# Offsets of the weight parts and the order of their matmuls in 55 gate and value units

## The chip, the cores and the metric

The kernel runs on one core of a Trainium2 chip. The metric is the device time in microseconds of one execution. The time before is the median of two runs.

## What is computed

One layer of a bidirectional encoder on 256 tokens of width 2048, in float32: an RMS norm, a combined projection, a windowed attention beside a Fourier mix, an output projection, and then the feed-forward part, with which this change deals. In the reference it reads:

```python
def _conv_ffn(h, w_up, dw_w, dw_b, w_down):
    up = h @ w_up
    gate, val = up[..., :D_FF], up[..., D_FF:]
    gate = lax.conv_general_dilated(
        gate, dw_w, window_strides=(1,), padding=((CONV_WIDTH // 2, CONV_WIDTH // 2),),
        dimension_numbers=('NWC', 'WIO', 'NWC'), feature_group_count=D_FF) + dw_b
    act = jax.nn.gelu(gate, approximate=False) * val
    return act @ w_down
...
x = x + _conv_ffn(_rmsnorm(x, norm2_g), w_up, dw_w, dw_b, w_down)
```

D_FF is 5504, which is 43 tiles of 128 features, so there are 43 gate tiles and 43 value tiles.

## The kernel before

Every float32 matrix is split in two parts of the type float32r: a high part, which ScalarE copies (L163), and a low part, which VectorE makes by subtracting the high part from the original (L164). A product is then the sum of high by high, high by low and low by high.

A **unit** is one tile of weights: for a gate or a value tile, 128 partitions by 2048 elements, which holds 16 stationary blocks of 128 by 128. `load` (L143) brings it in on SP's queue into one of three `raw` buffers. `split` (L156) makes its two parts in tiles `hi` and `lo`, three buffers each, 2176 elements wide, of which `parts_of` (L149) takes 2048 from an offset that the list `shifts` gives. The offset was 16 for the first eight units and 0 for all others.

`still_weights` (L303) multiplies a unit. The weights stand still in the array and the tokens move: `hk(k)` is block k of the normed, transposed input (the tiles `hU`), 512 elements wide, of which the first 256 are the high parts of the 256 tokens and the second 256 their low parts. First come 16 matmuls with the high weights on all 512 columns (L310), then 16 with the low weights on the first 256 columns (L313), all of them into one PSUM bank. ScalarE and VectorE add the two halves of the bank behind it (`scaled_sum`, L824 to L827), and the gate goes on through the convolution and the GELU.

The feed-forward part is a list of **items** (`ff_items`, L68): the gate and value units of tiles 0 to 7 first, then four groups that follow `PATTERN`: three units, then a down-projection product and a unit in turn. In it `u` is a unit and `s` a product (12 matmuls of 512 columns, `by_parts`, L1038), made for the tiles of the group before. After the groups come the last units and the rest of the down-projection. One loop (L1122) goes through the list. For each item it issues the matmuls and then `ff_step(n)`, which issues, in this order, the work on the item before (such as `scaled_sum`), the split of item n + 2 with the load that its buffer allows, and the work that may come behind. So the tiles of an item are written about two items ahead, and each of the two rings of three holds the item at work and the two that follow it. The order on each engine is written out by hand.

Of the kernel before, what the change touches and what calls it, by code (L numbers as in the profile page):

```python
# [13 lines left out]
P = 128  # L14
D = 2048
S = 256
NK = D // P
# [50 lines left out]
def ff_items():  # L68


    def ups(tiles):
        return [(kind, j) for j in tiles for kind in ("gate", "val")]

    items = ups(range(8))
    for g in range(N_GROUPS):
        todo = {
            "u": ups(range(8 * g + 8, 8 * g + 16)),
            "s": [("product", g, c, p) for c in range(2) for p in PRODUCTS[c]],
        }
        items += [todo[c].pop(0) for c in PATTERN]  # L80
        assert not any(todo.values())
    items += [("down", 0, c) for c in range(4)] + ups(LAST)
    items += [("down", 1, c) for c in range(4)] + [("last", c) for c in range(4)]
    return items
# [3 lines left out]
def block_kernel(  # L88
# [18 lines left out]
    nc = tc.nc  # L107
# [10 lines left out]
    def bank(pool, name):  # L118
        return pool.tile([P, 512], F32, tag=pool.name, name=name)
# [4 lines left out]
    shifts = [(SHIFT, SHIFT)] * 8 + [(0, 0)] * 32  # L124
    n_front = len(units)
    items, up_index = ff_items(), {}
    for n, it in enumerate(items):
        if it[0] == "product":
            continue
        up_index[n] = len(units)  # L130
        if it[0] in ("gate", "val"):
            units.append((w_up[2 * it[1] + (it[0] == "val")], 2048))
            shifts.append((0, 0))
            continue
        elif it[0] == "down":
            units.append((w_down_late[4 * it[1] + it[2]], 2048))
        else:
            units.append((w_down_last[it[1]], 512 * len(LAST)))
        shifts.append((0, 0))
    RAW = 3  # L140
    raws, halves = {}, {}
# [7 lines left out]
    def parts_of(i):  # L149
        halves[i] = tuple(  # L150
            wp.tile([P, 2176], F32R, tag=h, name=f"{h}{i}", bufs=3)[:, s : s + 2048]
            for h, s in zip(("hi", "lo"), shifts[i])
        )
        return halves[i]

# [43 lines left out]
    def u_part(k, o, n, m=1):  # L199

        rows = ux[k // 4][:, (k < 4) * U_HEAD :].rearrange("p (k c) -> p k c", k=4)
        return rows[:, k % 4 : k % 4 + m, o : o + n]
# [39 lines left out]
    ps = bank(dn, "ps_warm")  # L242
# [48 lines left out]
    def moving_weights(hi, lo, n, kk, act, b, ps, first, last, q0=0):  # L291

        for q, k in enumerate(kk, q0):
            ah = act(k)[:, b * P : (b + 1) * P]
            al = act(k)[:, S + b * P : S + (b + 1) * P]
            wh, wl = hi[:, q * n : (q + 1) * n], lo[:, q * n : (q + 1) * n]
            nc.tensor.matmul(ps, ah, wh, start=first and q == q0, stop=False)  # L297
            nc.tensor.matmul(ps, al, wh, start=False, stop=False)  # L298
            nc.tensor.matmul(  # L299
                ps, ah, wl, start=False, stop=last and q == q0 + len(kk) - 1  # L300
            )

    def still_weights(hi, lo, ps, kk):  # L303

        for k in kk:
            s = slice(k * P, (k + 1) * P)
            nc.tensor.matmul(ps, hi[:, s], hk(k), start=k == 0, stop=False)  # L310
        for k in kk:
            s = slice(k * P, (k + 1) * P)
            nc.tensor.matmul(  # L313
                ps[:, 0:S], lo[:, s], hk(k)[:, 0:S], start=False, stop=k == NK - 1
            )

    def hk(k):
        return hT[k // 4][:, k % 4, :]
# [18 lines left out]
    def at(when, i, f, *a):  # L337
        when.setdefault(i, []).append((f, a))
# [17 lines left out]
    for k in range(NK):  # L356
        c, q = k // 4, k % 4
        if q == 0:
            hi, lo = (t.rearrange("p (k c) -> p k c", k=4) for t in parts_of(c))
        n = 1 if c < 2 else 2  # L360
# [3 lines left out]
        if q % n == 0:  # L364
            w, h = u_part(k, 0, FW, n), hi[:, q : q + n, :]
# [3 lines left out]
        if k < 4:  # L369

            for p, w in enumerate([hi, hi, lo]):
                for b in range(2):
# [3 lines left out]
                        start=k == 0 and p == 0, stop=False,  # L376
# [405 lines left out]
    for n, (c, kq) in enumerate(OUT_ORDER):  # L782
        i = N_OUT + n
# [14 lines left out]
        if kq >= 2:  # L798
            part = "a" if kq == 2 else "f"
            ps = ps_a[c] if kq < 3 else ps_a[c, "f"]  # L800
# [113 lines left out]
    def ring_load():  # L914
        if ring_next[0] < len(ring):
            key = ring[ring_next[0]]
            ring_next[0] += 1
            ring_tiles[key] = fp.tile([P, 2048], F32, tag="rawd", name="rawd%d%d%s" % key)
            nc.sync.dma_start(ring_tiles[key], weights_of(*key))
# [24 lines left out]
    def first_sums(g, c):  # L944

        a, b = ring_tiles[g, c, "a"], ring_tiles[g, c, "b"]
        x = ring_tiles["x"] = fp.tile([P, 2048], F32, tag="sumw", name=f"sumw{g}{c}", bufs=1)
        nc.vector.tensor_tensor(x, a, b, ALU.add)
        nc.gpsimd.dma_start(b, weights_of(g, c, "d"), accum_op=ALU.add)
# [14 lines left out]
    def ff_step(n):  # L964
        todo, later[:] = list(later), []
        for f in todo:
            next(f, None)
        run(beside, n)
        split_item(n + 2)
        for f in todo:  # L970
            for _ in f:
                pass
        run(behind, n)

    def up_posts(n, kind, j, ps):
        if kind == "gate":
            at(beside, n + 1, scaled_sum, ps, f"g{j}")
            at(beside, n + 2, gate_conv, j)
            at(behind, n + 2, gate_gelu, j)
        else:  # L980
            at(beside, n + 1, scaled_sum, ps, f"v{j}")
            at(beside, n + 2, val_mult, j)
            if j % 8 == 7 and j < 8 * N_GROUPS:
                g = j // 8
                at(behind, n + 1, operand, g, "P1")
                at(behind, n + 2, operand, g, "N4")
                at(behind, n + 3, operand_sums, g, 0)
                at(behind, n + 4, operand, g, "P7")
                at(behind, n + 4, operand, g, "P2")
                at(behind, n + 5, operand_sums, g, 1)  # L990
                at(behind, n + 5, operand, g, "N5")
                at(behind, n + 6, operand, g, "N3")
                at(behind, n + 7, operand, g, "P6")
            if j >= 8 * N_GROUPS:
                at(behind, n + 2, act_parts, j)
# [42 lines left out]
    def by_parts(ps, o, hi, lo, first, last):  # L1038

        for p in range(4):  # L1040
            s = slice(p * 512, (p + 1) * 512)
            nc.tensor.matmul(ps, o[:, 0, p, :], hi[:, s], start=first and p == 0, stop=False)  # L1042
            nc.tensor.matmul(ps, o[:, 1, p, :], hi[:, s], start=False, stop=False)  # L1043
            nc.tensor.matmul(ps, o[:, 0, p, :], lo[:, s], start=False, stop=last and p == 3)  # L1044
# [59 lines left out]
    for q in range(2):  # L1104
        kind, j = items[q]
        ps = bank(mm, f"ps_{kind}{j}")
# [6 lines left out]
    for ps, hi, lo in pair:  # L1113
        still_weights(hi, lo, ps, range(12, NK))
# [7 lines left out]
    for n, it in enumerate(items):  # L1122
        if n < 2:
            continue
        if it[0] == "last":
            break
        if n in (8, 9):
            ring_load()
        if n == 13:
            pending.append(lambda: first_sums(0, 0))  # L1130
        if it[0] in ("gate", "val"):
            kind, j = it
            ps = bank(mm, f"ps_{kind}{j}")
            still_weights(*halves.pop(up_index[n]), ps, range(NK))
            ff_step(n)
            up_posts(n, kind, j, ps)
            continue
        if it[0] == "product":
            kind, g, c, p = it
            end = g == N_GROUPS - 1  # L1140
            if (c, p) in held:
                by_parts(held[c, p], parts[p], *halves.pop(it), g == 0, end)
            else:
                ps = bank(mm, f"ps_{p}{g}{c}")
                by_parts(ps, parts[p], *halves.pop(it), True, True)
                at(beside, n + 1, product_out, g, c, p, ps)
            if end and p == "N4":
                for q in range(3):
                    at(behind, n + 1 + q, shared_out, c, q)
        else:  # L1150
            kind, g, c = it
            hi, lo = halves.pop(up_index[n])
            ps = [bank(mm, f"ps_l{g}{c}{b}") for b in range(2)]
            for b in range(2):
                moving_weights(hi, lo, 512, LATE[g], act.get, b, ps[b], True, True)
            at(beside, n + 1, down_out, c, ps)
            if (g, c) == (0, 0):
                gfb = fp.tile([P, D], F32, tag="sumw", name="gfb", bufs=1)
                nc.gpsimd.dma_start(gfb, normf_g.partition_broadcast(P))
        ff_step(n)  # L1160
# [3 lines left out]
    i = up_index[n]  # L1164
# [149 lines left out]
```

## Time and profile before

| | us |
|---|---|
| median of the runs | 956.09 (955.68 to 956.5) |
| the profiled execution | 956.12 |
| its span | 954.4 |
| mean granted TensorE clock | 0.997 |

The span goes from the first to the last instruction of the profiled execution; the time also holds what lies around it. PE is TensorE's matmuls and PEld its weight loads, DVE is VectorE, ACT ScalarE, POOL GpSimd and SP the queue that issues most loads. L310 is line 310 of the kernel before. Times within the trace count from the start of the span. The feed-forward units begin at about 257 us and the four groups with products end at about 853 us. A matmul's record lasts longer than the distance to the next matmul, since matmuls are pipelined; the price of one in a stream is the distance from start to start.

### The profile page before, as it was taken

The numbers are of one execution on the slowest core, as the hardware profiler recorded it, in microseconds if no ns is written. First come the engines' busy times: TensorE is split into PE (matmuls) and PEld (weight loads), VectorE is DVE, ScalarE is ACT, GpSimd is POOL, SyncE is SP. The second block draws the span as 40 slices with busy tenths as digits, with TensorE's granted clock in tenths as the row PEclk, the third lists the DMA queues.
The fourth block names the chain that finished last, engine by engine and source line by source line (L and its number), as shares of the span: only waits on it lengthen the run. The fifth ranks groups of instructions, "written<-read, shape, count | busy, mean of one in ns | idle before, by whom it ended". The sixth has DMA issues, their size and how long they took to land.

```text
span 954.4 us, 12779 instructions
## 1 busy us (share of the span) xinstructions
PE 944.7 (99%) x5085; PEld 814.4 (85%) x5085; DVE 750.7 (79%) x935; ACT 534.2 (56%) x646; POOL 43.3 (5%) x58
## 2 busy tenths in 40 slices
PE   9999999999999999999999999999999999999996
PEld 7888998888888888888888888888888888888885
DVE  7658877566576689787898978988779979888775
ACT  7656766454454446556565555655556755554442
POOL 0000000000000000000000000000000000000003
PEclk9999999999999999999999999999999999999998
DMA  9844444446546676977778797876977687776442
GB/s 366 332 184 149 160 146 163 148 166 216 177 176 235 250 220 192 289 235 260 227 255 245 237 303 226 265 248 210 292 247 251 205 293 221 219 243 217 177 133 89
DMA packets 32108, 211.58 MB, mean 222 GB/s; under 512 B 3504, under 2 KB 4016, under 8 KB 7984
## 3 DMA queue, kind: packets, MB, share of 16 engines
q1 hardware_dynamic: 28448, 184.55, 52.2%
q0 software_dynamic: 3600, 26.22, 14.6%
q8 instruction: 40, 0.66, 0.3%
q14 instruction: 20, 0.16, 0.0%
HBM read 208.65 MB, written 2.10 MB: 221 GB/s over the span
## 4 chain that ended last, share of the span: by engine, by line
PE 98%; DVE 1%; DMA 0%; issue 0%; ACT 0%; POOL 0%; POOLq 0%; DVEq 0%; ACTq 0%
PE ps_gate L310 17%; PE ps_val L310 17%; PE ps_val L313 8%; PE ps_gate L313 8%; PE ps_q L310 5%; PE ps_P L1042 3%; PE ps_P L1043 3%; PE ps_P L1044 3%; PE ps_q L313 2%; PE ps_N L1042 2%; PE ps_N L1043 2%; PE ps_a L299 2%; PE ps_a L297 2%; PE ps_a L298 2%; PE ps_N L1044 2%; PE ps_k L310 2%
## 5 line engine op out<-in xcount | busy, mean ns | idle before, releaser
L164 DVE TENSOR_TENSOR lo<-raw,hi 128x2048 fp32r<-128x2048 f32 (+1 forms) x133 | 302.7, 2276 | 54.8 <-ACT hi L163 54.8
L163 ACT ACTIVATE hi<-raw 128x2048 fp32r<-128x2048 f32 (+1 forms) x133 | 253.1, 1903 | 59.9 <-PE ps_l L298 24.8
L310 PE MATMUL ps_gate<-hU,hi 128*128 128x512 f32 x688 | 165.5, 392 | 0.0
L310 PE MATMUL ps_val<-hU,hi 128*128 128x512 f32 x688 | 165.2, 392 | 0.0
L310 PEld LDWEIGHTS ps_gate<-hU,hi 128*128 128x128 f32 x688 | 128.1, 188 | 27.6
L310 PEld LDWEIGHTS ps_val<-hU,hi 128*128 128x128 f32 x688 | 128.0, 188 | 27.3
L313 PEld LDWEIGHTS ps_val<-hU,lo 128*128 128x128 f32 x688 | 85.4, 188 | 3.7
L313 PEld LDWEIGHTS ps_gate<-hU,lo 128*128 128x128 f32 x688 | 84.6, 188 | 3.8
L313 PE MATMUL ps_val<-hU,lo 128*128 128x256 f32 x688 | 86.2, 277 | 0.0
L824 ACT ACTIVATE ft_g<-ps_gate 128x256 f32<-128x256 f32 x43 | 16.5, 384 | 123.1 <-PE ps_gate L313 123.1
L313 PE MATMUL ps_gate<-hU,lo 128*128 128x256 f32 x688 | 85.2, 276 | 0.0
L824 ACT ACTIVATE ft_v<-ps_val 128x256 f32<-128x256 f32 x43 | 16.5, 385 | 92.7 <-PE ps_val L313 92.7
L1043 PE MATMUL ps_P<-hi_P,op_P 128*128 128x512 f32 x128 | 50.2, 392 | 0.0
L1042 PE MATMUL ps_P<-hi_P,op_P 128*128 128x512 f32 x128 | 50.1, 392 | 0.0
L1044 PE MATMUL ps_P<-lo_P,op_P 128*128 128x512 f32 x128 | 49.8, 389 | 0.0
L310 PE MATMUL ps_q<-hT,hi 128*128 128x512 f32 x192 | 46.5, 394 | 0.0
L934 DVE TENSOR_TENSOR lo_N<-sumw,hi_N 128x2048 fp32r<-128x2048 f32 x16 | 36.6, 2290 | 10.1 <-ACT hi_N L933 10.1
L310 PEld LDWEIGHTS ps_q<-hT,hi 128*128 128x128 f32 x192 | 35.2, 188 | 7.0
L826 DVE TENSOR_TENSOR fa_g<-ps_gate,ft_g 128x256 f32<-128x256 f32 x43 | 18.2, 423 | 26.1 <-ACT ft_g L824 26.1
L297 PE MATMUL ps_a<-hi,cat 128*128 128x512 f32 x96 | 37.9, 395 | 0.0
L1043 PE MATMUL ps_N<-hi_N,op_N 128*128 128x512 f32 x96 | 37.6, 392 | 0.0
L1042 PE MATMUL ps_N<-hi_N,op_N 128*128 128x512 f32 x96 | 37.6, 392 | 0.0
(332 smaller groups left out, 1561.4 us busy)
## 6 DMA issues: line engine op xcount, KB each, us to landing
raw<-in_w_up SPq DMA_DIRECT2D x86, 1024.0 KB, 5.2
raw<-in_w_in SPq DMA_DIRECT2D x20, 1024.0 KB, 4.8
raw<-in_w_out SPq DMA_DIRECT2D x16, 1024.0 KB, 4.9
sumw<-in_w_down POOLq DMA_DIRECT2D x16, 1024.0 KB, 8.7
raw<-in_w_down_late SPq DMA_DIRECT2D x8, 1024.0 KB, 4.8
raw<-in_w_down_last SPq DMA_DIRECT2D x4, 768.0 KB, 4.2
ux<-in_w_u_x SPq DMA_DIRECT2D x3, 768.0 KB, 9.3
xs<-in_x SPq DMA_DIRECT2D x4, 512.0 KB, 16.4
```

The source lines that it names most:

```text
L163: nc.scalar.activation(hi[:, 0:n], raw[:, 0:n], AF.Copy)
L164: nc.vector.tensor_tensor(lo[:, 0:n], raw[:, 0:n], f32(hi[:, 0:n]), ALU.subtract)
L297: nc.tensor.matmul(ps, ah, wh, start=first and q == q0, stop=False)
L298: nc.tensor.matmul(ps, al, wh, start=False, stop=False)
L299: nc.tensor.matmul(ps, ah, wl, start=False, stop=last and q == q0 + len(kk) - 1)
L310: nc.tensor.matmul(ps, hi[:, s], hk(k), start=k == 0, stop=False)
L313: nc.tensor.matmul(ps[:, 0:S], lo[:, s], hk(k)[:, 0:S], start=False, stop=k == NK - 1)
L824: nc.scalar.activation(tmp, ps[:, S : 2 * S], AF.Copy)
L934: nc.vector.tensor_tensor(lo, src, f32(hi), ALU.subtract)
L1042: nc.tensor.matmul(ps, o[:, 0, p, :], hi[:, s], start=first and p == 0, stop=False)
L1043: nc.tensor.matmul(ps, o[:, 1, p, :], hi[:, s], start=False, stop=False)
L1044: nc.tensor.matmul(ps, o[:, 0, p, :], lo[:, s], start=False, stop=last and p == 3)
```

## The change

The units that directly follow a down-projection product, 55 in number, each get an entry of a list `kinds`: the offset of the high part in its tile, the offset of the low part, a group size, and whether the order is turned in every second group. All other units, and the products, stay as they are. With a group size of `NK` (16) the order is the old one; with 2, two high matmuls are followed by the two low ones of the same blocks; with 1, high and low alternate. The low matmul of a block still uses 256 columns and the high one 512.

```diff
+    steps = (0, 16, 32, 48)
+    kinds = [(a, b, g, False) for g in (NK, 2, 1) for a in steps for b in steps]
+    kinds += [(0, 0, 1, True), (16, 0, 1, True), (0, 0, 8, False), (0, 0, 4, False)]
+    kinds += [(4, 4, NK, False), (60, 60, NK, False), (20, 20, NK, False)]
+    kind_of = {}
     for n, it in enumerate(items):
...
         if it[0] in ("gate", "val"):
             units.append((w_up[2 * it[1] + (it[0] == "val")], 2048))
-            shifts.append((0, 0))
+            if items[n - 1][0] == "product" and kinds:
+                kind_of[n] = kinds.pop(0)
+            shifts.append(kind_of.get(n, (0, 0)))
             continue
...
-            for h, s in zip(("hi", "lo"), shifts[i])
+            for h, s in zip(("hi", "lo"), shifts[i][:2])
...
-    def still_weights(hi, lo, ps, kk):
-        for k in kk:
-            s = slice(k * P, (k + 1) * P)
-            nc.tensor.matmul(ps, hi[:, s], hk(k), start=k == 0, stop=False)
-        for k in kk:
-            s = slice(k * P, (k + 1) * P)
+    def still_weights(hi, lo, ps, kk, group=NK, turn=False):
+        order = []
+        for n, k0 in enumerate(kk[::group]):
+            ks = range(k0, min(k0 + group, kk[-1] + 1))
+            for w in (lo, hi) if turn and n % 2 else (hi, lo):
+                order += [(w, k) for k in ks]
+        for n, (w, k) in enumerate(order):
+            x = slice(0, S if w is lo else 2 * S)
             nc.tensor.matmul(
-                ps[:, 0:S], lo[:, s], hk(k)[:, 0:S], start=False, stop=k == NK - 1
+                ps[:, x], w[:, k * P : (k + 1) * P], hk(k)[:, x],
+                start=n == 0 and k == 0, stop=n == len(order) - 1 and k == NK - 1,
             )
...
-            still_weights(*halves.pop(up_index[n]), ps, range(NK))
+            still_weights(
+                *halves.pop(up_index[n]), ps, range(NK), *kind_of.get(n, (0, 0, NK, False))[2:]
+            )
```

An offset counts elements of four bytes.

## The prediction

> **What bounds the kernel now.** I read the page first, then what TensorE waited for, then the chain of waits around the changed units, then single stretches of the timeline.
>
> ```profile
> span 954.4 us, 12779 instructions
> ...
> PE 944.7 (99%) x5085; PEld 814.4 (85%) x5085; DVE 750.7 (79%) x935; ACT 534.2 (56%) x646; POOL 43.3 (5%) x58
> ...
> PEclk9999999999999999999999999999999999999998
> ...
> PE 98%; DVE 1%; DMA 0%; issue 0%; ACT 0%; POOL 0%; POOLq 0%; DVEq 0%; ACTq 0%
> ```
>
> TensorE is busy for 99% of the span at a full granted clock, and 98% of the chain that ended last is its own matmuls. Its waits, all of them:
>
> ```profile
> PE ps_warm L244 <- POOL ones L236: 1.0, 1, 1.0
> PE ps_u L374 <- ACT hT L251: 0.2, 1, 0.2
> ```
>
> After the start it waits for nobody, so only two things can move the time: the distance from one matmul's start to the next, and a new wait. The change touches 55 of the 86 gate and value units. The chain of waits shows five groups of matmuls, with start, length and count:
>
> ```profile
> 352.74 3.66 PE ps_val L310 x16
> 356.40 1.88 PE ps_val L313 x16
> 358.28 3.68 PE ps_gate L310 x16
> 361.96 1.81 PE ps_gate L313 x16
> ...
> 366.52 3.68 PE ps_val L310 x16
> 370.20 1.81 PE ps_val L313 x16
> ```
>
> L310 is the product with the high parts (512 columns), L313 the one with the low parts (256 columns). The unit at 366.52 follows a down-projection product, as all 55 do. It takes 3.68 + 1.81 = 5.49 us: 230.0 ns for a high matmul, 113.1 ns for a low one, 343.1 ns for a pair of the two. The unit at 352.74 follows another unit, does the same work with tiles at the same offsets, and has 228.8 and 117.5 ns. So one shape has more than one price, and the price depends on what ran before. That is the ground on which this change plays. Two neighbouring streams bound it:
>
> ```profile
> 133.88 0.71 PE ps_o L688 x6
> 134.60 0.72 PE ps_s L616 x6
> ...
> 852.66:874.42 21.76, 21.76 (x97) 18.02 (x96) 21.13 (x23) 8.10 (x6) 0.00 (x0) 1.00 0.65 228
> ```
>
> The first two rows (chain of waits) are 256-column matmuls of the attention, 118.3 and 120 ns each. The third is a stretch of 96 matmuls of 512 columns into ps_l (97 touch it): us, then each engine's busy time, and 21.76 / 96 = 226.7 ns, the shortest steady price that I see for that width.
>
> ```profile
> 500.76 0.39 PE L1044 MATMUL ps_P<-lo_P,op_P 128*128 128x512 f32 x1
> 500.99 1.10 PE L310 MATMUL ps_gate<-hU,hi 128*128 128x512 f32 x4
> ...
> 501.93 0.62 PE L310 MATMUL ps_gate<-hU,hi 128*128 128x512 f32 x2
> ```
>
> This is the timeline of a unit that starts behind a product: its first four high matmuls begin at 500.99 and the fifth at 501.93, which is 235 ns each. The start of a new stream is its slowest part.
>
> **The change part by part.** It adds no instruction and removes none: each unit keeps 16 high and 16 low matmuls of the same widths, one ScalarE copy, one VectorE subtraction and one load. The 55 units, by their list: 16 keep the old order with offsets of 0, 16, 32 or 48 elements of the high and the low part (the first of these is the old unit); 16 with the same offsets go in groups of two high, two low; 16 alternate high and low; two alternate with the order turned in every second pair; one goes by eights, one by fours; three keep the order with offsets of 4, 60 and 20. So 34 units, 34 x 16 = 544 pairs, are interleaved, and 20 others are changed in the offset or hardly in the order.
>
> Offsets, on the writers:
>
> ```profile
> L164 DVE TENSOR_TENSOR lo<-raw,hi x3: 2292/2293/2293, 24.4 to 37.7; 128x2048 fp32r<-128x2048 f32 x3
> ...
> L163 ACT ACTIVATE hi<-raw x4: 1901/1911/1918, 22.4 to 39.2; 128x2048 fp32r<-128x2048 f32 x4
> ...
> L164 DVE TENSOR_TENSOR lo<-raw,hi x15: 2281/2284/2293, 370.4 to 477.6; 128x2048 fp32r<-128x2048 f32 x15
> ...
> L163 ACT ACTIVATE hi<-raw x15: 1902/1913/1924, 367.4 to 473.5; 128x2048 fp32r<-128x2048 f32 x15
> ```
>
> The rows are minimum, median and maximum ns. Before 40 us the tiles already stand at offset 16, after 366 us at 0: the medians are 2293 against 2284 and 1911 against 1913 ns. I cost an offset of whole sixteens at nothing there. TensorE's lack of waits hides a few ns more.
>
> Offsets, on the reader: no row shows a stationary operand at another offset. The bounds are the two prices of a low group, 1.81 and 1.88 us. All 55 units have the lower one now, so an offset can hardly help there and can cost 0.07 us a unit. I take one unit in four flipped: 20 x 0.07 / 4 = 0.35 us, with 0 and 1.4 as ends. The offsets of 4, 60 and 20 have no near row; their three units stand in the same term.
>
> Interleaving, the new wait: the low part is needed at the second or third matmul of a unit instead of the seventeenth.
>
> ```profile
> 497.48 2.29 DVE L164 TENSOR_TENSOR lo<-raw,hi 128x2048 fp32r<-128x2048 f32 x1
> ```
>
> This low part is complete at 499.77, and its unit starts at 500.99. It is 1.22 us early, the tightest of the 55 that I found. The move costs nothing. If VectorE came 1.3 us later, each unit would wait, with the next matmuls of TensorE, and everything after, queued behind.
>
> Interleaving, the release of tiles: the high tile is now read until the end of its unit, about 1.8 us longer.
>
> ```profile
> L824 ACT ACTIVATE ft_g<-ps_gate 128x256 f32<-128x256 f32 x43 | 16.5, 384 | 123.1 <-PE ps_gate L313 123.1
> ```
>
> The next writer of that tile is ScalarE's copy for the item three places on. It is issued behind L824, which itself waits for the unit's last matmul, as its row says. So ScalarE could not use the earlier release, and nothing is lost. The loads on SP's queue keep their order and hang on the same copies and subtractions; GpSimd's accumulating loads hang on the products' tiles, which don't change.
>
> Interleaving, on the array: before, a unit had one switch from high to low; now it has 31 (alternating), 15 or 16. What a switch does to the weight load is seen at the old borders:
>
> ```profile
> 358.01 3.52 PEld L310 LDWEIGHTS ps_gate<-hU,hi 128*128 128x128 f32 x16
> ...
> 358.12 3.84 PE L310 MATMUL ps_gate<-hU,hi 128*128 128x512 f32 x16
> ```
>
> Here a high matmul follows the last low one. Its weights begin to load 0.11 us ahead, which is the whole length of that low matmul, and the matmul starts as soon as it ends. The short matmul still covers the load, so no load is uncovered by alternating. What is left is the price of each matmul in a stream that keeps switching: for the high ones between 226.7 and 235 ns, for the low ones between 113.1 and 120 ns, a pair between 339.8 and 355 ns against 343.1 now. That is -1.8 to +6.5 us over 544 pairs. I take the high ones as they are, and the low ones half way between the two prices of their own group, 115.3 ns, because the lower one has so far come only in an unbroken run of low matmuls: 2.2 x 544 = 1.2 us.
>
> **Sum.** +1.2 + 0.35 = +1.55 us on the profiled execution's 956.12 us, whose span is 954.4, with 1.7 us around it that nothing here touches. It lies 0.03 us from the median of the runs, 956.09. I forecast 957.7 us.
>
> **The rivals.** *Order and offset don't matter* (chance 0.17): the load and the stream don't meet, the times of the changed units stay 5.49 us, and the kernel stays at 956.1. For it: the writers' rows, and the border at 358. Against it: the same group at 1.81 and 1.88 us. The Trainium skill says this outright ("TensorE: Matmul & The Clock Gate", section "Step-by-step: what each phase is for"): TensorE has two independent read ports, so that loading the next tile's weights takes no read bandwidth from the running matmul. By that rule a matmul's price would be fixed by its columns; this case's trace has 226.7 to 235 ns for 512 of them, so I don't follow it for the small terms.
>
> *The streams fall into step* (0.17): both kinds of matmul go at their shortest, 16 x 226.7 ns + 1.81 us = 5.437 us a unit instead of 5.49. The gain is 0.053 x 55 = 2.9 us: 953.2. For it: the ps_l run stays at 226.7 with a new pair of operands at each step. Against it: 16 high matmuls in a row never reach it now.
>
> *Every switch is a start* (0.12): high matmuls stay at the 235 ns of a unit's beginning and low ones at 120. 11.9 x 544 = 6.5 us, and the offsets' upper end 1.4: 964.0. This is slower than before, by 0.8%. For it: the first matmuls behind a product are the slow ones. Against it: the unit at 352.74 begins after a low group and has the lower 3.66 us.
>
> *The load of the high weights is laid bare* (0.02): if a high load could not run beside a low matmul, each pair would pay the 0.11 us between the load at 358.01 and its matmul at 358.12: 0.11 x 544 = 59.8 us, 1015.9. This is the rival of the other sign that passes 2%. It decides from 19.1 / 544 = 35 ns of uncovered load per pair. The rows at 358 speak against it.
>
> The forecast has 0.52, its own range 955.9 to 961. To leave out no more than two in ten I take half of the falling-into-step case and half of the every-switch case in: 954.0 to 962.5. Two per cent, about what a measurement of this kernel can tell from no change, is 19 us: only the laid-bare load passes it, 0.02; for a gain of that size no case is left, 0.01 for what I don't see; within it 0.97.
>
> **What would show it.** Right: the interleaved units at 5.45 to 5.65 us, the low matmuls among them spaced between 113 and 120 ns, no wait of TensorE behind L164, and most units of the old order at 5.49 or 5.54 whatever their offset. In-step shows as 5.44 us in most units, every-switch as 5.68. Wrong: a unit beyond 5.7 us, TensorE waiting for VectorE or ScalarE, or offsets of one kind that all lie apart from the others.

## The result, and the profile after

The changed kernel takes 961.50 us (961.50 to 961.51, two runs), against 956.09 before: a ratio of 1.0056, with a 95% interval of 1.004 to 1.0072. That is a slowdown of half a per cent, far inside the two per cent, and 5.4 us where the forecast had 1.6. The time lies inside the stated 954.0 to 962.5 us, and 0.5 us above the forecast's own range of 955.9 to 961. The profiled execution also took 961.50 us.

The page after:

```profile
span 959.7 us, 12779 instructions
...
PE 950.0 (99%) x5085; PEld 818.9 (85%) x5085; DVE 750.7 (78%) x935; ACT 534.2 (56%) x646; POOL 43.4 (5%) x58
...
PE 98%; DVE 1%; DMA 0%; issue 0%; ACT 0%; POOL 0%; POOLq 0%; DVEq 0%; ACTq 0%
```

The instructions are as many as before, VectorE and ScalarE are busy exactly as long, and the 5.3 us of the span stand on TensorE alone (944.7 before). Its waits:

```profile
PE ps_warm L253 <- POOL ones L245: 1.0, 1, 1.0
PE ps_u L388 <- ACT hT L260: 0.3, 1, 0.3
```

No wait was added. So the matmuls themselves stand further apart. The two matmul lines of `still_weights` have become one, L326, and the chain of waits now merges the 32 matmuls of a unit into one piece (start, length, what). The pieces shown are, in order: old order with offsets 0/0, 0/16, 0/32, 16/0, 16/16 and 32/16 (high/low); twos with 0/0; alternating with 0/0, 0/16 and 0/32; and the last one, old order with 20/20.

```profile
366.82 5.50 PE ps_val L326 x32
...
375.06 5.60 PE ps_gate L326 x32
...
383.41 5.51 PE ps_val L326 x32
...
399.99 5.55 PE ps_val L326 x32
...
408.29 5.58 PE ps_gate L326 x32
...
441.62 5.66 PE ps_gate L326 x32
...
511.23 5.55 PE ps_val L326 x32
...
655.80 5.59 PE ps_val L326 x32
...
664.13 5.46 PE ps_gate L326 x32
...
672.34 5.54 PE ps_val L326 x32
...
849.89 5.52 PE ps_val L326 x32
```

The first unit is the old unit and has the old length. Nearly all others are longer, the ones that kept their order too. All 48 that combine the four offsets, in us from the unit's first matmul to the next item's:

| order | high offset | low 0 | low 16 | low 32 | low 48 |
|---|---|---|---|---|---|
| old | 0 | 5.495 | 5.599 | 5.508 | 5.577 |
| old | 16 | 5.553 | 5.583 | 5.557 | 5.602 |
| old | 32 | 5.628 | 5.656 | 5.631 | 5.636 |
| old | 48 | 5.600 | 5.636 | 5.543 | 5.611 |
| twos | 0 | 5.554 | 5.590 | 5.630 | 5.603 |
| twos | 16 | 5.549 | 5.570 | 5.595 | 5.604 |
| twos | 32 | 5.548 | 5.679 | 5.575 | 5.619 |
| twos | 48 | 5.622 | 5.645 | 5.624 | 5.596 |
| alternating | 0 | 5.588 | 5.461 | 5.539 | 5.550 |
| alternating | 16 | 5.599 | 5.549 | 5.564 | 5.595 |
| alternating | 32 | 5.636 | 5.470 | 5.639 | 5.611 |
| alternating | 48 | 5.655 | 5.624 | 5.563 | 5.600 |

Over 5.495 us, the 16 of the old order cost 1.50 us together, the twos 1.68, the alternating ones 1.32, the other seven 0.43. That is 4.93 of the 5.4 us; the products behind the units add 0.1, and the feed-forward part began 0.3 us later than in the profile of before, behind a part that the change leaves alone.

Where a unit's time goes is seen in the timeline, for units with 0/0, 0/16, 16/0 and 20/20 in the old order (start, length, and the start of the product behind them):

```profile
366.66 3.84 PE L326 MATMUL ps_val<-hU,hi 128*128 128x512 f32 x16 
370.34 1.98 PE L326 MATMUL ps_val<-hU,lo 128*128 128x256 f32 x16 
...
372.16 0.39 PE L1056 MATMUL ps_P<-hi_P,op_P 128*128 128x512 f32 x1 
...
374.90 3.84 PE L326 MATMUL ps_gate<-hU,hi 128*128 128x512 f32 x16 
378.58 2.08 PE L326 MATMUL ps_gate<-hU,lo 128*128 128x256 f32 x16 
...
380.50 0.39 PE L1056 MATMUL ps_N<-hi_N,op_N 128*128 128x512 f32 x1 
...
399.83 3.83 PE L326 MATMUL ps_val<-hU,hi 128*128 128x512 f32 x16 
403.50 2.04 PE L326 MATMUL ps_val<-hU,lo 128*128 128x256 f32 x16 
405.38 0.39 PE L1056 MATMUL ps_P<-hi_P,op_P 128*128 128x512 f32 x1 
...
849.73 3.79 PE L326 MATMUL ps_val<-hU,hi 128*128 128x512 f32 x16 
853.36 2.05 PE L326 MATMUL ps_val<-hU,lo 128*128 128x256 f32 x16 
855.25 0.39 PE L1056 MATMUL ps_N<-hi_N,op_N 128*128 128x512 f32 x1 
```

The high matmuls take 3.68 us in the first two, the low ones 1.82 with the low part at 0 and 1.92 at 16. The unit with 20/20 has its high ones at 3.63 us, 226.7 ns each, which is the shortest steady price of before, but its low ones at 1.89. So each offset moves its own half of the unit, up or down. The low half depends on the high offset as well: with 16/0 the low part is at 0 again, as in the old unit, and its matmuls take 1.88 us instead of 1.82.

### The profile page after: what moved, and what is told of

It is laid out like the page before. It is cut to its first block, busy times and chain, and to the rows that moved or that the text cites. A ratio compares the mean times of both kernels' runs of the same rounds, so it can differ in the third digit from the quotient of the medians.

```text
span 959.7 us, 12779 instructions
## 1 busy us (share of the span) xinstructions
PE 950.0 (99%) x5085; PEld 818.9 (85%) x5085; DVE 750.7 (78%) x935; ACT 534.2 (56%) x646; POOL 43.4 (5%) x58
## 4 chain that ended last, share of the span: by engine, by line
PE 98%; DVE 1%; DMA 0%; issue 0%; ACT 0%; POOL 0%; POOLq 0%; DVEq 0%; ACTq 0%
PE ps_val L326 25%; PE ps_gate L326 25%; PE ps_q L326 7%; PE ps_P L1056 3%; PE ps_P L1057 3%; PE ps_P L1058 3%; PE ps_k L326 2%; PE ps_N L1056 2%; PE ps_N L1058 2%; PE ps_N L1057 2%; PE ps_a L308 2%; PE ps_a L306 2%; PE ps_a L307 2%; PE ps_l L307 2%; PE ps_l L308 2%; PE ps_l L306 2%
## 5 line engine op out<-in xcount | busy, mean ns | idle before, releaser
L326 PE MATMUL ps_gate<-hU,hi 128*128 128x512 f32 x688 | 190.9, 393 | 0.0
L326 PE MATMUL ps_val<-hU,hi 128*128 128x512 f32 x688 | 190.5, 393 | 0.0
L326 PEld LDWEIGHTS ps_gate<-hU,hi 128*128 128x128 f32 x688 | 123.6, 188 | 22.1
L326 PEld LDWEIGHTS ps_val<-hU,hi 128*128 128x128 f32 x688 | 123.6, 188 | 22.1
L326 PE MATMUL ps_val<-hU,lo 128*128 128x256 f32 x688 | 117.8, 280 | 0.0
L326 PE MATMUL ps_gate<-hU,lo 128*128 128x256 f32 x688 | 117.4, 279 | 0.0
L326 PEld LDWEIGHTS ps_gate<-hU,lo 128*128 128x128 f32 x688 | 103.6, 188 | 9.3
L326 PEld LDWEIGHTS ps_val<-hU,lo 128*128 128x128 f32 x688 | 103.9, 188 | 8.9
L326 PE MATMUL ps_q<-hT,hi 128*128 128x512 f32 x192 | 46.5, 394 | 0.0
L326 PEld LDWEIGHTS ps_q<-hT,hi 128*128 128x128 f32 x192 | 35.2, 188 | 7.0
L1056 PE MATMUL ps_N<-hi_N,op_N 128*128 128x512 f32 x96 | 37.6, 392 | 0.0
L1058 PE MATMUL ps_N<-lo_N,op_N 128*128 128x512 f32 x96 | 37.6, 391 | 0.0
```

What stands on the lines that cost most here:

```text
L326: nc.tensor.matmul(ps[:, x], w[:, k * P : (k + 1) * P], hk(k)[:, x], start=n == 0 and k == 0, stop=n == len(order) - 1 and k == NK - 1,)
```

## The experiments

Three questions were open: whether offsets or order cost the time, whether a unit's time is its own or comes from its neighbours, and what about an offset counts. Unless said otherwise, unit times and prices of a matmul are distances from start to start in the trace of the run. A **rhythm** is a sequence of such distances that repeats, and **dear** and **cheap** stand for long and short. Times of kernels are medians; where an interval is given, the ratio is to the kernel before on the same chip. The kernels for which no time is given ran once, and only their traces are read.

**Offsets alone, order alone.** In the first kernel all 55 units have the old order, in the second all have offset 0.

```diff
+    kinds = [(a, b, NK, False) for a, b, g, t in kinds]
```

> All 55 units keep the old order, each with the offsets of its entry. If a unit's time is its own, set by its offsets and its order wherever it stands, the 16 offset pairs cost what they cost in the trace of the changed kernel (together 1.50 us over 16 old units), now three times, with 0.24 us for the rest: 956.1 + 4.7 = 960.8 us, and the pair of offsets 0 and 16 is again about 5.60 us a unit. If the switches between high and low cost the time, only the 19 units that had kept the order stay dear: 957.8 us.

```diff
+    kinds = [(0, 0, g, t) for a, b, g, t in kinds]
```

> All 55 units at offset 0, each in the order of its entry. If a unit's time is its own, the units in twos cost 0.06 us and the alternating ones 0.09 us over 5.495, as the ones at offset 0 do in the trace of the changed kernel, and with the last few the sum is 2.7 us: 958.8 us. If only the offsets cost the time: 956.1 us.

With the offsets alone 961.17 us (ratio 1.0053, 1.0038 to 1.0068), with the order alone 958.81 (1.003, 1.0017 to 1.0043). Both came out as a sum of the units' own prices: 960.8 and 958.8 were expected. The chain of the first:

```profile
366.74 5.50 PE ps_val L327 x32
...
374.98 5.60 PE ps_gate L327 x32
...
391.58 5.58 PE ps_gate L327 x32
```

Offset pairs of the table (0/0, 0/16, 0/48), with the same times; later in that run, where the changed kernel had its twos, each pair takes within 1 ns of these again. In the second run every unit in twos takes 5.554 us and every alternating one 5.588, to 1 ns, at every place. So offsets cost time without any new order, a new order costs time without any offset, and neither needs the other. The theory that only switches between high and low cost falls, and so does the one that only offsets do.

**A scan of the offsets.** Old order throughout, but for four alternating units near the end.

```diff
-    kinds = [(a, b, g, False) for g in (NK, 2, 1) for a in steps for b in steps]
...
+    kinds = [(a, 0, NK, False) for a in range(0, 64, 4)]
+    kinds += [(20, b, NK, False) for b in range(0, 64, 4)]
+    kinds += [(a, 0, NK, False) for a in (64, 80, 84, 96, 100, 112, 17, 18, 19, 21, 22, 23)]
+    kinds += [(16, 48, NK, False), (0, 0, NK, False), (20, 20, NK, False), (32, 16, NK, False)]
+    kinds += [(0, 16, 1, False), (32, 16, 1, False), (20, 20, 1, False), (20, 0, 1, False)]
...
```

> Old order; the high offset goes from 0 to 60 in steps of 4, then the low one with the high one at 20, then offsets of 64 and more and single steps from 17 to 23; four units alternate. If the place of a weight block counts within 256 bytes (64 elements), offsets 64, 80, 84, 96 and 112 have the high prices of 0, 16, 20, 32 and 48, and 20 with 0 takes 16 x 226.7 ns and 1.81 to 1.88 us: 5.44 to 5.51 us a unit. If only what ran before counts and the place does not, all units of the old order go at 5.49 or 5.54 us, whatever their offsets. Alternating units at 0 and 16 or 32 and 16 take 5.46 to 5.47 us again, if the time is their own.

The high matmuls' price runs from 226.6 ns (offset 20) to 234.3 (offset 23) with no plain trend: 230.1 at 0, 228.4 at 12, 229.2 at 16, 233.9 at 32, 229.9 at 60. Offsets 64, 80, 84, 96, 100 and 112 repeat 0, 16, 20, 32, 36 and 48 to 0.1 ns. The two units with 20 and with 84 in the timeline:

```profile
407.61 3.79 PE L328 MATMUL ps_gate<-hU,hi 128*128 128x512 f32 x16 
411.24 1.93 PE L328 MATMUL ps_gate<-hU,lo 128*128 128x256 f32 x15 
...
670.55 3.79 PE L328 MATMUL ps_val<-hU,hi 128*128 128x512 f32 x16 
674.17 2.04 PE L328 MATMUL ps_val<-hU,lo 128*128 128x256 f32 x16 
```

Both have their high ones in 3.63 and 3.62 us. So the place of a block counts within 256 bytes, as the first theory has it. The alternating units with 0/16 and 32/16 take 5.462 and 5.469 us, as expected. A multiple of 64 bytes is nothing special: 20 elements, 80 bytes, are the best high offset here, and 32 elements, 128 bytes, one of the worst. But the best half doesn't make the best unit: with the high part at 20 the low matmuls are at 117.8 ns or so, and the unit takes 5.510 us at a low offset of 0 and 5.496 at best, at 4. In the old order no pair that was tried beats offsets of 0.

**The moving operand moved.** As with the offsets alone, and the tiles that stream stand 16 elements on; the weight tiles are 64 elements narrower to make room.

```diff
-        t = base.tile([P, 4, 512], F32R, tag=f"hT{c}", name=f"hU{c}")
+        t = base.tile([P, 2112], F32R, tag=f"hT{c}", name=f"hU{c}")[:, 16:2064]
+        t = t.rearrange("p (k c) -> p k c", k=4)
```

> As the kernel with the offsets only, but the moving operand itself stands 16 elements on in its tile. If the distance between the block that is loaded and the block that streams sets the price, a unit with offsets a and b has the price that a - 16 and b - 16 (modulo 64) had: 16 and 16 take 5.495 us with low matmuls at 113.3 ns, 0 and 0 take the 5.61 us of 48 and 48. If the place of the weights alone sets it, 0 and 0 stay at 5.495 us and 16 and 16 at 5.58 us.

```profile
367.94 5.63 PE ps_val L327 x32
...
409.71 5.55 PE ps_gate L327 x32
...
442.97 5.51 PE ps_gate L327 x32
```

The chain shows the units with 0/0, 16/16 and 32/16. The old unit has become dear (5.626 us, where the distance theory expected 5.61), so the place of the weights alone doesn't set the price. The unit with 16/16 comes at 5.548, not at 5.495: here the expectation failed. Single starts show what holds and what doesn't. The rhythm into which the high matmuls settle has moved by 16: at 0 it was 226, 229, 232 ns in turn, and now it is that at 16; at 16 it was a steady 227, and now at 32; at 32 it was 236, 231, and now at 48. The low ones' 120 ns at offset 16 are now at 32. What has not moved along is the entry into the unit: the unit with 0/0 began with high matmuls of 236, 235, 232 and 232 ns, and the one with 16/16, now at the same distance, begins with 230, 229, 232 and 226; its low ones then settle at 117.8 instead of 113.3. So the distance between the block that loads and the block that streams, within 256 bytes, sets which rhythms there are, which this run shows for a move of 16 elements; that the entry decides among them is the reading that fits. The trace of before bears it out. Behind a product the low matmuls go at 113.3 ns, and behind another unit at 113.3 and 117.8 in turn, always at the same offsets. In all 84 whole units of that trace the price goes with the point at which the rhythm 226, 229, 232 breaks off: where the last high distance is 231 or 232 ns the low ones take 113, and where it is 225 or 226 they take 118. No run set this point on purpose.

**A scan of alternating units.**

```diff
+    kinds = [(0, b, 1, False) for b in range(0, 64, 4)]
+    kinds += [(32, b, 1, False) for b in range(0, 64, 4)]
+    kinds += [(a, 16, 1, False) for a in range(0, 64, 4)]
...
```

> Nearly all of the 55 units alternate; the low offset goes from 0 to 60 in steps of 4 with the high one at 0, then with it at 32, then the high one with the low one at 16. In an alternating unit the low weights load beside a high matmul and the high weights beside a low one. If a matmul's price is set by the block that loads beside it, the prices cross over: the high matmuls follow the low offset, close to 226.7 ns at 12, 16 and 20 whatever the high offset, and the low ones follow the high offset, 113 or 118 ns at 0 and 32. If a matmul's own weights set its price, the high matmuls keep one price while only the low offset changes.

```profile
400.23 5.46 PE ps_val L327 x32
...
408.43 5.68 PE ps_gate L327 x32
...
536.30 5.47 PE ps_gate L327 x32
...
544.53 5.47 PE ps_val L327 x32
```

The four are 0/16, 0/20, 32/12 and 32/16. With the high offset fixed at 0 the high price moves from 227.6 (low offset 16) to 236.4 ns (20), so a high matmul does pay for the low block beside it, and its own weights alone don't set its price. But the neat crossing over failed: with the low offset at 12 and 20 the high ones were to be near 226.7 and are, with the high offset at 0, at 231.7 and 236.4, and the low price moves along with the low offset too, from 113.8 to 121.4. So the two halves of a pair can't be priced apart, and the long runs of one kind don't predict them.

**One good pair of offsets, in 55 units and in all.** For the second kernel the queries and keys alternate as well.

```diff
+    kinds = [(0, 16, 1, False)] * 55
```

> All 55 units alternate with offsets 0 and 16. If a unit's time is its own, each takes 5.46 us against 5.495: 55 x 0.034 = 1.8 us less than before, 954.3 us. If alternating costs by its switches, the unit of 5.46 us was a chance of its neighbours, and the time is 958 us or more.

```diff
+    kinds = [(0, 16, 1, False)] * 86
...
-            if items[n - 1][0] == "product" and kinds:
+            if n > 1 and kinds:
...
+    shifts = [(SHIFT, SHIFT)] * 8 + [(0, 16)] * 16 + [(0, 0)] * 16
...
+            still_weights(hi, lo, ps, range(NK), 1)
```

> The same for all gate and value units but the first two and for the 16 units of queries and keys. The units that follow another unit take 5.49 and 5.54 us in turn before; at 5.46 us they give 1.7 us more, the queries and keys about 0.9 us: 951.6 us. If an alternating unit leaves a bad start for the unit that follows it directly, those units lie above 5.5 us and the time is about that of the kernel with 55, 954 us.

The first takes 954.33 us (ratio 0.9979, 0.9971 to 0.9988), as expected to 0.03 us: a unit has 30 more switches than before, and is faster. The second takes 954.63 us (0.9985, 0.9976 to 0.9994), 3 us above its expectation. Its chain:

```profile
350.17 5.60 PE ps_gate L323 x32
...
369.74 5.46 PE ps_val L323 x32
...
476.42 5.46 PE ps_gate L323 x32
481.88 5.44 PE ps_val L323 x32
487.32 5.44 PE ps_gate L323 x32
```

All alternate with the same offsets. The units before the first product take 5.60 us each (the first of them 5.68), 232 and 118 ns in turn from the first to the last matmul. The first unit behind a product starts in the same way (232, 118, 227, 120), and then falls to 226.7 and 113.3. Units that follow such a one directly start there and take 5.44 us, the floor of the forecast's second rival. So the same work has two rhythms, 350 and 340 ns a pair, and in this stretch a unit that directly follows another keeps the rhythm that it finds.

**The rhythm handed on.** The first kernel alternates only behind the first product. The second puts eight different units before the alternating ones of the early part.

```diff
+            if n > 18 and kinds:
```

> Alternating with offsets 0 and 16 in all units behind the first product; the units before it, and the queries and keys, keep the old order at offset 0. If the cheap state of an alternating unit is carried into the next unit, as in the trace of the kernel where all alternate, the six units that open the later groups and the six last ones go at 5.44 us: 0.9 us less than with the 55 alone, 953.4 us. If the directly following units fall into the dear state of 5.60 us, as the early ones of that kernel did, the time is about 955 us.

```diff
+    X = (0, 16, 1, False)
+    before_x = [(0, 0, NK), (32, 16, 1), (20, 20, NK), (0, 20, 1), (32, 12, 1), (20, 0, NK), (0, 16, NK), (0, 16, 2)]
+    kinds = [k for a, b, g in before_x for k in ((a, b, g, False), X)] + [X] * 70
```

> As the kernel where all units alternate, but among the early units eight different ones stand in turn before one that alternates at 0 and 16. If the price of such a unit is a state that is taken over from the unit before, some of these eight take 5.44 to 5.47 us and others 5.60, and what follows the cheap ones is cheap. If it is the place in the kernel (the early part, with its fuller DMA queues), all eight take 5.60 us.

953.26 us for the first (0.9968, 0.9956 to 0.9981), as expected. The early part of the second, unit by unit (each second one in the sequence, from 275.59 on, is 0/16; the others are the eight):

```profile
270.10 5.49 PE ps_gate L325 x32
275.59 5.44 PE ps_val L325 x32
...
291.91 5.63 PE ps_gate L325 x32
297.54 5.45 PE ps_val L325 x32
302.98 5.44 PE ps_gate L325 x32
...
324.74 5.62 PE ps_gate L325 x32
330.36 5.60 PE ps_val L325 x32
335.96 5.59 PE ps_gate L325 x32
341.55 5.60 PE ps_val L325 x32
```

Six of the 0/16 units behind them are cheap, at 5.44 to 5.46 us, and two dear. Behind an old unit (270.10) or one with 20/20 (291.91) the next unit is cheap; behind 20/0 (324.74) or the old order with 0/16 (335.96) it is dear. All eight stand in the early part, with the same loads, so the early part as such is out; what ran before decides. The unit at 302.98 shows how far this goes: it alternates with 0/20, which behind a product was the dearest of the scan at 5.68 us, and behind a cheap unit it takes 5.44. So the prices in the tables hold for units behind a product, and belong to an offset pair together with what runs in front of it.

**The faster version, and one step too far.** One old unit first, then all gate and value units alternate; and the same with nine of the queries' and keys' units.

```diff
+    kinds = [(0, 0, NK, False)] + [(0, 16, 1, False)] * 85
...
+            if n > 1 and kinds:
```

> All gate and value units from the fourth on alternate with offsets 0 and 16; the third keeps the old order at offset 0, behind which the cheap state came. If the state is handed on from unit to unit, the 16 units before the first product take 5.44 us each instead of 5.49 and 5.54 in turn, 1.2 us less than with only the later ones: 952.0 us. If it is lost on the way, they lie at 5.60 us and the time is 954 us or more.

```diff
+    ALT = (1, 3, 5, 6, 7, 9, 11, 13, 15)
+    shifts = [(SHIFT, SHIFT)] * 8 + [(0, 16 * (n in ALT)) for n in range(16)] + [(0, 0)] * 16
...
+            still_weights(hi, lo, ps, range(NK), 1 if n in ALT else NK)
```

> The same, and nine of the 16 units of queries and keys alternate, those that had the cheap state when all alternated. If the unit or product before them decides, as it did there, 0.5 us less: 951.4 us. If their cheap state hung on their neighbours alternating too, some take 5.68 us instead of 5.45 and nothing is gained.

The first takes 952.17 us (ratio 0.996, 0.9947 to 0.9972), as expected to 0.2 us, and has the lowest median of all. Its early units, behind the old one:

```profile
269.62 5.49 PE ps_gate L323 x32
275.11 5.44 PE ps_val L323 x32
```

The second takes 952.38 us (0.997, 0.9958 to 0.9982) and gains nothing: three of the nine units now lie at 5.60 us and one at 5.69, where with all of them alternating they had 5.44 or 5.55. Their cheap rhythm hung on their neighbours, as the second theory had it, though three of the four take 5.60 us where that theory had 5.68.

**The moving operand moved, alternating.** The edit of the moved kernel, and

```diff
+    kinds = [(16, 32, 1, False), (0, 16, 1, False)] * 28
```

> The moving operand stands 16 elements on in its tile, and the 55 units alternate with offsets 16 and 32 or 0 and 16 in turn. If the distance between weights and moving operand decides, the units at 16 and 32 settle at 226.7 and 113.3 ns a matmul, about 5.46 us, and those at 0 and 16 lie at 5.53 us or more. If the place of the weights alone decides, it is the units at 0 and 16 that take 5.46 us.

```profile
367.96 5.60 PE ps_val L323 x32
...
376.28 5.65 PE ps_gate L323 x32
```

Neither took 5.46 us. The units at 16/32 go at 233 and 117 ns in turn, 350 a pair: that is the dear rhythm of 0/16. The units at 0/16 go at 233 and 120, which without the move was the rhythm of 48/0 (5.655 us in the table), 16 elements back. So the distance again sets the rhythms and the place of the weights alone doesn't; that the entry chose the dear one of the two is the reading that fits, since no run here made the moved pair go at 340. The expectation left the entry out, and failed there.

## Why the forecast was right in sign and small in size

**The range.** The forecast was +1.55 us and the kernel lost 5.4. It stays inside the stated range only because half of the every-switch case was taken in, and the mechanism of that case did not come true; the forecast's own range was missed by 0.5 us. That the range held is in part luck.

**The bound.** Right: TensorE waits for nobody, and all of the change stands in the distance between matmuls.

**The parts costed at nothing.** Right: the writers at shifted offsets (VectorE's busy time is the same 750.7 us), the low part needed earlier, the later release of the high tile, the weight load at a switch. TensorE's two waits are those of before, and alternating 55 units is even faster when the offsets fit. Two readings behind these were loose and did no harm. The tightest low part of before was not 1.22 us early but 0.9: it is written from 750.60 to 752.88, and its unit starts at 753.78. And the load at 358.01 is recorded with 0.188 us, so by its record it ends 0.07 us behind the start of its matmul; the short matmul does not cover it whole, and still no unit paid the 0.11 us a pair of the laid-bare case.

**The offsets' term.** This failed most for its size: 0.35 us from "one unit in four flipped", ends 0 and 1.4. The 20 units cost 1.80 us, which is above the upper end: 1.50 for the offset pairs, 0.18 for the odd offsets, 0.12 for the orders by eights and fours. Most of it is the step "one unit in four". Of the 15 changed units with offset pairs, 13 have low matmuls of 117.8 ns or more, and only 0/32 and 48/32 stay near the lower price, at 114.1; the low halves cost 1.16 of the 1.50 us. The size of a flip was low too: the two prices in the trace of before were taken as the range of a low group, 0.07 us a unit, while other distances have others, up to 120.4 ns. The rest, 0.34 us, is a term that was left out: the high half has a price by offset of its own, from 229.2 to 233.9 ns in these units, of which the trace of before showed nothing, since all its units stood at one distance.

**The interleaving's term.** 1.2 us expected, 3.13 measured in the 34 units (1.68 for twos, 1.32 alternating, 0.13 turned). The term was for the order, and these units have offsets too. With all offsets at 0, in the second kernel of the experiments, the same 34 orders cost 2.55 us; so the order alone cost twice its term, 4.7 ns a pair against 2.2, and the offsets added about 0.6 us that stood in no term. The low matmuls came at 117.7 ns on average in both orders, not at 115.3, and the high ones, taken as unchanged at 230.0, at 232.3 in twos and 230.9 alternating. The reason given for the low half, that its lower price had come only in an unbroken run, is not the one that the runs showed: 113.3 ns also came in perfect alternation. A pair between 339.8 and 355 ns held as a bound for the averages of all these units: the cheapest unit has 341.3 and the dearest 354.9.

**The rivals.** That order and offset don't matter is refuted, by the offsets alone (1.0053) and the order alone (1.003). With it falls what the prediction drew from the Trainium skill's rule ("TensorE: Matmul & The Clock Gate", section "Step-by-step: what each phase is for"), that a matmul's price would be fixed by its columns: 512 columns took 225 to 241 ns within the one unit in twos with 0/16, and the offsets alone changed the time. Whether a load takes read bandwidth from the running matmul, which is what the rule itself denies, no run here shows. Falling into step happened in two of the 55 units (0/16 and 32/16, alternating) and, made general, it is the faster version; its price of 5.44 us a unit is met by the units that directly follow another, while those behind a product take 5.46. Every switch a start did not come true as a mechanism: the dearest units lie where it put them, but the old order, with its one switch, is among them (32/16, 5.656 us). The laid-bare load did not appear.

**What would show it.** The interleaved units were put at 5.45 to 5.65 us: 32 of the 34 are within that, one at 5.655 and one at 5.679 above. The low matmuls of the 34 average 113.8 to 120.2 ns a unit, against 113 to 120. "Most units of the old order at 5.49 or 5.54 whatever their offset" was wrong. And the last of the signs of being wrong, offsets of one kind that lie apart, all but happened: with the high part at 32 the old order takes 5.628 to 5.656 us, and of all others in that order only 48/16, at 5.636, comes up to them.

Open: which part of the chip makes the distance count. The runs show a period of 256 bytes and the dependence on both operands; nothing in them tells one part of the chip from another.

## What to carry to other kernels

Where TensorE is the bound and its matmuls are float32r as here, the place of the stationary block against the streaming one can be worth changing: in this kernel it moved a unit of the old order by up to 3% (5.495 to 5.656 us), and the best arrangement found gained 0.4% of the whole time. Measure unit by unit, and keep the pair that settles at the shortest distance. A price that depends on the neighbours can't be moved with the unit: check a good variant in the sequence in which it will run, and think of the entry, since one unit before it can decide for all that follow. When a trace shows two prices for one shape, don't take them for the ends of a range: here they were two of many. And a count that no row bears out, as the one unit in four was here, is a guess and sizes its term as one.

## What the runs showed of the hardware

Two rhythms of the same instructions at the same offsets, 340 and 350 ns a pair, each kept over sixteen units in a row (5.44 us in the kernel with one old unit first, 5.60 where all alternate). And prices that repeat to a nanosecond: the same unit in the offsets-only kernel, three times in one run, has the same length to 1 ns. So where each unit kept its neighbours, the units' prices from one trace added up to the next kernel's time within 0.4 us (960.8 expected and 961.17 measured, 958.8 and 958.81, 954.3 and 954.33); where the neighbours changed, the sum could miss by 3 us (951.6 and 954.63).
